# A hybrid four-branch layer on one core: another order of channel tiles, and weights' low parts on VectorE

## The chip, the core and the metric

One Trainium2 chip, of which one core is used. A core has a matrix engine (TensorE, PE), three engines for elementwise work (VectorE or DVE, ScalarE or ACT, GpSimd or POOL) and SyncE (SP), on which most transfers are issued. Each engine runs its own instructions in order; semaphores hold it where it needs another's result. The metric is the device time of one execution in microseconds (us); lower is better.

## The reference

One decoder layer on 2048 prompt tokens with 16 meta tokens ahead of them, and on 8 sample sequences of 4 tokens with saved states. The residual is normalised, then multiplied with a matrix of 1024 rows whose columns feed four branches and their gates:

```python
u = jnp.einsum('btd,de->bte', x, lw['w_in'])
(z_a, xbc, dt_raw, z_b, u_b, z_c, qkv, b_raw, a_raw,
 z_d, q_d, f_d, i_d) = _split_last(u, _IN_SIZES)
```

Branch A is a chunked state-space scan after a causal convolution of 4 taps over `xbc`. Branch B is a diagonal complex scan over `u_b`. Branch C is a gated delta rule: `qkv` goes through a convolution of 4 taps, q and k are L2-normalised per head, and each chunk needs the inverse of a triangular matrix. Branch D is a linear recurrence with a forget gate made of `f_d`. Every branch's result is multiplied by SiLU of its own columns z; the four are joined, multiplied with an output matrix, added to the residual and normalised. All final states are returned too.

## The kernel before, in words

**Stages.** The tokens go through in two halves: 48 (samples and meta tokens) and eight chunks of 128 in the first, eight chunks in the second. Per half, phase 1a normalises and transposes the input and makes the token-major products; phase 1b (`phase1b`, `proj`) makes the other columns, 22 channel tiles of 128 columns. After both halves comes the output phase, 17 chunks in which the last chunks of branches A and C are mixed with the output products.

**A channel tile.** Float32 accuracy is had from two parts of each operand, high and low. `wload` loads a tile's weights (512 KB) into `wr`, of which there is one buffer, copies the high part on ScalarE (L579) and subtracts it on GpSimd for the low part (L580). The next tile's `wload` is called ahead of a tile, and `w` has two buffers, so the parts for tile j+1 can be written once tile j-1 is done. The products run over token blocks of 304, 384 and 384 in the first half, and two of 512 in the second; each block is eight steps of three products (high by high, high by low of x, low of w by high), so 24 products.

**What takes a tile's result.** `conv_tile` (k and q of branch C, v, and x): ScalarE copies the block out (L628 to L635), GpSimd makes the last tap (L639), VectorE adds three more (L641), ScalarE applies SiLU. For k and q the job `l2n` then sums squares (L681, L683), takes a power on GpSimd (L695), scales (L697) and transposes the norm on TensorE. `stream_out` (q, f of branch D, all z): ScalarE only, then a store.

**Order.** The tile order is a list in `phase1b`: k k b b q q l l f f v v x x x x c c a a d d, one letter a tile. k and l are the two pairs of k and q of branch C's convolutions, b c a d the gate columns z of these branches, q and f branch D's, v and x convolutions. The dependent chains (gates, norms, branch B in `right_jobs` and `b_main`, branch D, branch C's inverses) are generators, jobs, that yield an estimate in us of when their next step can start. `poll` is called between the products of `proj` and lets a job go on when the estimate says so. TensorE executes in the order in which this weaving writes it (`keep_in_program_order`); the instructions of the other engines are put in order by the framework's scheduler.

**The hook `last`.** It runs as the first thing of one tile, in place of that tile's own hook: it drains what is left of branch C's inverses, closes the convolutions' buffers, and in the first half starts the second half's input; in the second half it also drains branch D (`right`) and starts the jobs of the remaining chunks (`head`, `c_invs`, `chunks`). Before, that is the first c tile, number 16 counted from 0.

**Branch B.** `b_main` multiplies two arrays of about 1024 columns by cosines on VectorE (L1141, L1150) and their swapped copies, which come by DMA, by sines on GpSimd (L1142, L1151), for four pieces in all. Its setup (`bs_wt`, L1070 to L1072) and the doubling that makes the tables (L956 to L961) run on VectorE early in the first half.

Of the kernel before, what the change touches and what calls it, by code (L numbers as in the profile page):

```python
# [22 lines left out]
F32 = mybir.dt.float32  # L23
# [27 lines left out]
KORD = [0, 1, 4, 5, 6, 7, 2, 3]  # L51
HEAD = META + NS
# [18 lines left out]
class Pinned:  # L71
    """An engine whose instructions don't move ahead of earlier ones."""
# [8 lines left out]
class Chain:  # L81
    """An engine whose instructions issued through here stay in the order in which they are written."""
# [14 lines left out]
class Kern:  # L97
# [12 lines left out]
    # The tensor engine runs in the order in which the kernel is written out. Dependent chains  # L110
    # are generators ("jobs") that yield the time until their next step can start; they are
    # woven between the matrix products of the projections.
# [64 lines left out]
    # ---------------------------------------------------------------- constants  # L177
    def consts(self, cp):
        nc, V, S, G = self.nc, self.V, self.S, self.G
        a = self.a  # L180
# [13 lines left out]
        # sums the two parts of 32 channels of a head  # L194
# [24 lines left out]
    # ---------------------------------------------------------------- phase 1  # L219
    def small_loads(self, cp):  # L220
        """Job: small parameters, and the conv histories of the sample sequences channel-major."""
        a, V = self.a, self.Vp
        yield 8.2
        # channel-major small parameters, through one transpose
# [29 lines left out]
        # HGRN2 lower bound: softmax over the single layer, cumulative sum minus the first entry  # L254
# [18 lines left out]
        for i1 in range(0, 10, 6):  # L273
# [4 lines left out]
            yield 8.5  # L278
# [46 lines left out]
    def phase1a(self, half, xp):  # L325
        """Layer norm and transposition of the input, and the products whose results are wanted token-major.
        The first yield comes before anything that needs the space of xh, xl or the weight ring."""
# [46 lines left out]
        def weights(i, parts):  # L374
            """u | i, dt, a, b: high and low parts."""
# [23 lines left out]
        else:  # L399
            # the first tile waits for as little as possible: one row comes by DMA, the other through the tensor engine  # L400
# [81 lines left out]
    def gates_in(self, half, sp):  # L482
# [3 lines left out]
        o = 1 - half          # chunk 0, the tail, is the first of half 0  # L486
# [14 lines left out]
        # softplus = max(x, 0) + log1p(e), log1p(e) = 2 atanh(e / (2 + e))  # L501
# [20 lines left out]
        # beta = sigmoid  # L522
# [7 lines left out]
        # inclusive cumulative sums inside each chunk, and the chunk totals  # L530
# [20 lines left out]
        if o:  # L551
            # decays of the tail segments, on every partition
# [8 lines left out]
        # rows: 0-7 cumulative logs, 8-15 their exponentials  # L561
# [12 lines left out]
    def wload(self, c0):  # L574
        S, V = self.S, self.V
        w = self.wp.tile([128, 8, 256], F32R, name="w0", bufs=2).rearrange("p k (j c) -> p k j c", j=2)
        raw = self.wp.tile([128, DM], F32, name="wr", bufs=1).rearrange("p (k c) -> p k c", c=128)
        self.ld(raw, self.a["w_in"][0, :, c0:c0 + 128].rearrange("(k p) c -> p k c", p=128))
        S.copy(w[:, :, 0], raw)  # L579
        self.G.tensor_tensor(w[:, :, 1], raw, w[:, :, 0].bitcast(F32), SUB)  # L580
        return w

    def proj(self, tiles):
        """tiles: (first column, per-block consumer, hook at the start); the next tile's weights are made ready first."""
# [20 lines left out]
    def conv_tile(self, i, c0, dst=None, nrm=None):  # L605
        """Causal conv and SiLU of one 128-channel tile, block by block.
        The first block is laid out as 8 x (3 history, 4 sample) | 3 zeros | meta | prompt."""
# [54 lines left out]
    def l2n(self, st, dst, scale, nd, need, key):  # L662
        """Job: L2 normalisation over the channels of a head, for the blocks of a conv tile."""
# [22 lines left out]
        yield 6.1  # L686
# [31 lines left out]
    def decay(self, pool, tag, t, rows0, nh, bufs=None):  # L718
        """exp(acum_i - acum_j) for i >= j of one segment, 0 elsewhere, as [j, head, i]."""
# [10 lines left out]
    def c_pre(self, p):  # L730
        """Job: decayed K K^T and Q K^T of two heads, transposed."""
# [29 lines left out]
    def base_inv(self):  # L761
        """Inverses of the diagonal blocks of I + M, one block to a partition: 32 x 32 in the
        prompt chunks, 16 x 16 in chunk 0, whose segments don't cross multiples of 16."""
# [34 lines left out]
    def stream_out(self, c0, outs, mark=None):  # L798
        """outs: list of (function of (dst, psum)), dram destination)."""
# [18 lines left out]
    def phase1b(self, half, last):  # L818
# [29 lines left out]
        c0, use, _ = zc[0]  # L848
        zc[0] = (c0, use, last)
        tiles = kq[0:2] + zb + qd + kq[2:4] + fd + v + xbc + zc + za + zd  # L850
        yield from self.proj(tiles)

    def conv_states(self):
        """Job: the conv states that go out."""
# [11 lines left out]
    # ---------------------------------------------------------------- branch B  # L866
    def exp_acc(self, pool, dst, x):
        """dst = exp(x) in float32 accuracy, for small tiles."""
# [20 lines left out]
    def b_setup(self, bp, tp):  # L889
# [56 lines left out]
        # powers of lambda, d = 0..8  # L946
# [21 lines left out]
        # rotating frame over chunks of 8  # L968
# [38 lines left out]
        # input matrices  # L1007
# [28 lines left out]
        # output matrices: Xc = (Cr | -Ci), Yc = (-Ci | -Cr)  # L1036
# [25 lines left out]
        # W1 = in-state matrices [(j q), (re n | im n)]  # L1062
# [15 lines left out]
        # block Toeplitz  # L1078
# [17 lines left out]
        # signed multipliers for single steps: h' = re * h + im_s * swap(h)  # L1096
# [17 lines left out]
    def b_main(self, blk, bp, tp):  # L1114
# [8 lines left out]
        for hq in range(2):  # L1123
            yield 4.7 - 95.9 * hq
# [6 lines left out]
        for gh in range(2):  # L1131
            yield 2.0 - gh
# [9 lines left out]
        G.tensor_tensor(Vs, Vs, self.sinT[:, :, 1:65], MUL)  # L1142
# [8 lines left out]
        G.tensor_tensor(Gs, Gs, self.sinT, MUL)  # L1151
# [4 lines left out]
        for hq in range(2):  # L1156
# [14 lines left out]
            yield 2.8 + 0.7 * hq  # L1171
# [112 lines left out]
    # ---------------------------------------------------------------- chunks  # L1284
# [865 lines left out]
```

## Time and profile before

| | us |
|---|---|
| three runs | 1452.39, 1443.35, 1450.69 |
| median | 1450.69 |
| span of the profiled execution | 1448.2 |
| TensorE busy in it | 1294.9 |
| VectorE busy | 934.2 |
| GpSimd busy | 616.3 |
| ScalarE busy | 536.1 |

The profiled execution is given by its span, the time from its first instruction to its last; no other time of it is listed. Its mean granted TensorE clock is 0.936 of full speed. In a row of the trace, L580 is line 580 of the kernel before; names are those of the program, with the tile written left of the arrow.

### The profile page before, as it was taken

The page shows a single profiled execution, that of the slowest core. Times are in us where ns is not written, and L with a number is a line of the kernel's source. Part 1 is how long each engine was busy: PE and PEld are TensorE (multiplying, and loading weights), DVE is VectorE, ACT ScalarE, POOL GpSimd, SP SyncE. Part 2 cuts the span into 40 slices and gives each one's busy share as a digit, 9 for nine tenths or more (in the row PEclk, how much of TensorE's full clock was granted, in tenths as well). Part 3 has the DMA queues.
Part 4 walks back from the last instruction along what each step waited for, and adds up shares of the span by engine and source line. Part 5 has one row for each costly group of instructions (what it writes and reads, how often), then busy time and mean ns, then how long its engine had stood idle before and what let it go on. Part 6 is the DMA issues. An engine that isn't in the chain of part 4 may idle for free. (4 is left out here: it accounts for less than half of the span.)

```text
span 1448.2 us, 23800 instructions
## 1 busy us (share of the span) xinstructions
PE 1294.9 (89%) x8596; PEld 1090.3 (75%) x8596; DVE 934.2 (65%) x2173; ACT 536.1 (37%) x1010; POOL 616.3 (43%) x508
## 2 busy tenths in 40 slices
PE   7984898899898999998996888789997999999997
PEld 6974788878877999877674677677775677777776
DVE  8899524557978549474355789962345676665654
ACT  3224256545214342353543442242434332333211
POOL 4065322524433312152434443441324476676665
PEclk9997999999989999999998899899998899999999
DMA  8511552464337434215534633125649777676333
GB/s 211 192 49 36 127 143 57 140 189 114 106 97 203 145 104 153 77 39 158 157 87 121 201 102 95 44 88 145 177 124 251 196 198 190 198 182 184 111 105 113
DMA packets 259007, 195.79 MB, mean 135 GB/s; under 512 B 70950, under 2 KB 231928, under 8 KB 258873
## 3 DMA queue, kind: packets, MB, share of 16 engines
q1 hardware_dynamic: 258890, 194.28, 47.2%
q8 instruction: 68, 1.11, 0.3%
q14 instruction: 49, 0.39, 0.1%
HBM read 125.01 MB, written 64.31 MB: 131 GB/s over the span
## 5 line engine op out<-in xcount | busy, mean ns | idle before, releaser
L126 PE MATMUL pj<-xh,w 128*128 128x384 f32 (+2 forms) x1760 | 547.8, 379 | 10.8 <-ACT raw L635 5.5
L126 PEld LDWEIGHTS pj<-xh,w 128*128 128x128 f32 x1760 | 339.7, 200 | 57.4 <-issue 11.6
L126 PE MATMUL pj<-xl,w 128*128 128x384 f32 (+2 forms) x880 | 322.8, 367 | 0.0
L126 PEld LDWEIGHTS pj<-xl,w 128*128 128x128 f32 x880 | 176.3, 200 | 12.4 <-issue 0.5
L580 POOL TENSOR_TENSOR w<-wr,w 128x1024 fp32r<-128x1024 f32 x44 | 109.9, 2497 | 85.6 <-ACT w L579 68.0
L641 DVE SCALAR_TENSOR_TENSOR cv<-raw,par,cv 128x384 f32<-128x384 f32 (+2 forms) x150 | 130.5, 872 | 9.5 <-POOL cv L639 8.2
L126 PE MATMUL pj<-woh,o_mh 128*128 128x512 f32 (+2 forms) x280 | 116.6, 416 | 6.3 <-DVE xt L1846 3.2
L126 PE MATMUL pj<-wol,o_mh 128*128 128x512 f32 (+2 forms) x280 | 109.4, 391 | 6.2 <-POOL wol L1817 5.9
L126 PE MATMUL pj<-woh,o_ml 128*128 128x512 f32 (+2 forms) x280 | 109.4, 391 | 0.0
L126 PE MATMUL pj<-w,xh 128*128 128x256 f32 (+3 forms) x544 | 105.2, 295 | 0.0
L639 POOL TENSOR_SCALAR cv<-raw,par 128x384 f32<-128x384 f32 (+2 forms) x50 | 49.3, 986 | 119.0 <-ACT raw L635 95.4
L126 PEld LDWEIGHTS pj<-w,xh 128*128 128x128 f32 (+1 forms) x544 | 84.6, 189 | 1.2 <-ACT xh L88 0.8
L126 PE MATMUL pj<-w,xl 128*128 128x256 f32 (+3 forms) x272 | 78.0, 291 | 0.8 <-DVE xl L88 0.8
L725 POOL TENSOR_TENSOR cdec<-cdec,negm 128x256 f32<-128x256 f32 x32 | 29.4, 921 | 98.6 <-DMA cdec<-rows_d 63.1
L126 PEld LDWEIGHTS pj<-woh,o_mh 128*128 128x128 f32 (+1 forms) x280 | 52.3, 187 | 18.6 <-DVE xt L1846 4.0
L126 PEld LDWEIGHTS pj<-wol,o_mh 128*128 128x128 f32 (+1 forms) x280 | 52.5, 188 | 16.0 <-POOL wol L1817 6.9
L1789 DVE TENSOR_TENSOR y<-y,f_R 128x768 f32<-128x768 f32 (+1 forms) x17 | 27.1, 1591 | 56.0 <-POOL f_R L1788 50.9
L126 PEld LDWEIGHTS pj<-woh,o_ml 128*128 128x128 f32 (+1 forms) x280 | 52.2, 187 | 12.3 <-issue 0.7
L308 POOL TENSOR_TENSOR lnrs<-lnve,mhalf 128x1 f32<-128x1 f32 (+1 forms) x34 | 24.5, 720 | 74.0 <-DVE lnve L88 46.2
L813 ACT ACTIVATE zs<-pj 128x384 f32<-128x384 f32 (+2 forms) x40 | 20.8, 520 | 87.6 <-PE pj L126 72.8
L126 PEld LDWEIGHTS pj<-w,xl 128*128 128x128 f32 (+1 forms) x272 | 51.2, 190 | 1.5 <-DVE xl L88 1.3
L1788 POOL TENSOR_TENSOR f_R<-f_R,f_z 128x768 f32<-128x768 f32 (+1 forms) x17 | 30.2, 1778 | 51.1 <-DMA f_R<-r_d 32.5
(570 smaller groups left out, 2687.8 us busy)
## 6 DMA issues: line engine op xcount, KB each, us to landing
wr<-in_w_in_dram SPq DMA_DIRECT2D x46, 512.0 KB
xt<-in_x_prompt_dram SPq DMA_DIRECT2D x16, 512.0 KB
xn_d<-xt SPq DMA_DIRECT2D x16, 512.0 KB
ma<-cma SPq DMA_DIRECT2D x64, 128.0 KB
xt<-xn_d SPq DMA_DIRECT2D x16, 512.0 KB
out_dram<-xt SPq DMA_DIRECT2D x15, 512.0 KB
f_R<-r_d SPq DMA_DIRECT2D x32, 192.0 KB
cdec<-rows_d SPq DMA_DIRECT2D x32, 128.0 KB
```

Source lines behind the costliest of these rows:

```text
L126: self._pe(self.PE.matmul(out, lhsT, rhs, start=start, stop=stop, **kw), 0.01 + n * (1 if rhs.dtype == F32R else 4) / 2400)
L308: self.G.tensor_tensor(rs[:n], ve[:n], self.mhalf[:n, 0:1], ALU.pow)
L580: self.G.tensor_tensor(w[:, :, 1], raw, w[:, :, 0].bitcast(F32), SUB)
L639: G.tensor_scalar(cv[:, 0:m], raw[:, 3:3 + m], w[3], b, op0=MUL, op1=ADD)
L641: V.scalar_tensor_tensor(cv[:, 0:m], raw[:, k:k + m], w[k], cv[:, 0:m], op0=MUL, op1=ADD)
L725: G.tensor_tensor(d[:n, :, :n], d[:n, :, :n], m[:n, None, :n].to_broadcast([n, nh, n]), ADD)
L813: S.activation(z, p, AF.Silu)
L1788: G.tensor_tensor(R[:, :, :n], R[:, :, :n], z[:, :, :n], MUL)
L1789: V.tensor_tensor(y6[:, 0:6, :n], y6[:, 0:6, :n], R[:, :, :n], MUL)
```

## The change

The two tile orders become tables, one string per half, and the hook gets a place of its own: tile 17, the second c tile, in both halves. The first half starts with a q tile of branch D, an x tile comes right behind the l tiles, and its end is c c a d d a. The second half differs in its end alone, c c a d d a. The subtraction that makes the weights' low part, and the two products with the sines, are issued on VectorE in place of GpSimd. Three estimates in jobs change (the yields below; those of `b_main` keep their values but for one, which was negative and is now 0).

```diff
+ORDER = ["qkkbbqllxffvvxxxccadda", "kkbbqqllffvvxxxxccadda"]
+LAST = [17, 17]
...
-            yield 8.5
+            yield 9.2
...
-        self.G.tensor_tensor(w[:, :, 1], raw, w[:, :, 0].bitcast(F32), SUB)
+        V.tensor_tensor(w[:, :, 1], raw, w[:, :, 0].bitcast(F32), SUB)
...
-        yield 6.1
+        yield 9.0 if half else 6.1
...
-        c0, use, _ = zc[0]
-        zc[0] = (c0, use, last)
-        tiles = kq[0:2] + zb + qd + kq[2:4] + fd + v + xbc + zc + za + zd
+        groups = {"a": za, "b": zb, "c": zc, "d": zd, "q": qd, "f": fd, "k": kq[0:2], "l": kq[2:4], "v": v, "x": xbc}
+        tiles = [groups[g].pop(0) for g in ORDER[half]]
+        c0, use, _ = tiles[LAST[half]]
+        tiles[LAST[half]] = (c0, use, last)
...
-            yield 4.7 - 95.9 * hq
+            yield 0.0 if hq else 4.7
...
-        G.tensor_tensor(Vs, Vs, self.sinT[:, :, 1:65], MUL)
+        V.tensor_tensor(Vs, Vs, self.sinT[:, :, 1:65], MUL)
...
-        G.tensor_tensor(Gs, Gs, self.sinT, MUL)
+        V.tensor_tensor(Gs, Gs, self.sinT, MUL)
```

In instructions: VectorE's order gets 52 operations more, 44 low parts and 8 products with sines, and GpSimd's as many fewer. The lines of the changed kernel are 2 higher than before from L52 on and 4 higher from about L850.

**VectorE, first half, up to the last of branch B's four setup sums** (`bs_wt` of 512 columns; L641 becomes L643, L1072 becomes L1076, and TensorE transposes each sum). Before:

```order
L960 TENSOR_TENSOR bs_l<-sinT,bur 128x256
L960 TENSOR_TENSOR bm_1371<-bui,bur 128x16
L683 TENSOR_REDUCE l2p<-sq 128x2
L641 SCALAR_TENSOR_TENSOR cv<-raw,par,cv 128x384
L1070 TENSOR_TENSOR bs_wt<-bs_X,bpr 128x128 x4
L694 TENSOR_SCALAR l2r<-pq 128x18
L671 MEMSET l2p 128x4
L961 TENSOR_TENSOR sinT<-sinT,bs_l 128x16x16
L961 TENSOR_TENSOR bvi<-bvi,bm_1371 128x16
L681 STREAM_TRANSPOSE sq<-acc 128x256
L641 SCALAR_TENSOR_TENSOR cv<-raw,par,cv 128x384
L1072 TENSOR_TENSOR bs_wt<-bs_wt,bs_wu 128x512
```

and now:

```order
L1075 TENSOR_TENSOR bs_wu<-bs_Y,bpi 128x128 x2
L964 TENSOR_TENSOR bs_l<-sinT,bur 128x256
L963 TENSOR_TENSOR sinT<-cosT,bui 128x16
L643 SCALAR_TENSOR_TENSOR cv<-raw,par,cv 128x384
L1074 TENSOR_TENSOR bs_wt<-bs_X,bpr 128x128 x4
L685 TENSOR_REDUCE l2p<-sq 128x8
L634 COPY cst<-raw 128x24
L965 TENSOR_TENSOR sinT<-sinT,bs_l 128x16x16
L999 COPY bur<-bvr 128x16
L636 COPY raw<-raw 128x3
L643 SCALAR_TENSOR_TENSOR cv<-raw,par,cv 128x328
L1076 TENSOR_TENSOR bs_wt<-bs_wt,bs_wu 128x512
```

Ahead of the second of these sums there stood 10 taps of convolutions (L641), and now 4 (L643); ahead of the third 15 and 7, ahead of the last 18 and 10. Of the 44 low parts (L582), 4 now stand ahead of the last sum. On TensorE the four transposes stand among the same products of tiles 0 to 2 as before, the last of them three products later.

**GpSimd and VectorE, second half, around one call of `b_main`** (`w_...` is a tile's weights, `cdec` and `cma` belong to branch C's decayed products). GpSimd before:

```order
L580 TENSOR_TENSOR w_6631<-wr,w_6631 128x8x128
L695 TENSOR_TENSOR l2r<-l2r,mhalf 128x16
L580 TENSOR_TENSOR w_6761<-wr,w_6761 128x8x128
L725 TENSOR_TENSOR cdec<-cdec,negm 128x256
L580 TENSOR_TENSOR w_6952<-wr,w_6952 128x8x128
L725 TENSOR_TENSOR cdec<-cdec,negm 128x256
L1142 TENSOR_TENSOR b_6934<-b_6934,sinT 128x1024
L725 TENSOR_TENSOR cdec<-cdec,negm 128x256 x2
L1151 TENSOR_TENSOR b_6944<-b_6944,sinT 128x1040
L725 TENSOR_TENSOR cdec<-cdec,negm 128x256 x2
L580 TENSOR_TENSOR w_7116<-wr,w_7116 128x8x128
```

VectorE now, the same call:

```order
L582 TENSOR_TENSOR w_6748<-wr,w_6748 128x8x128
L1716 SCALAR_TENSOR_TENSOR SD<-SD,d_tota,pq 64x64 x4
L696 TENSOR_SCALAR l2r<-pq 128x16
L1144 COPY b_6910<-bH_1937 128x16
L699 TENSOR_SCALAR l2r<-l2r 128x16
L1125 COPY b_6806<-b_6803 128x8x8x16
L704 COPY l2s<-pq 16x128
L715 TENSOR_TENSOR acc<-acc,bc 128x536
L715 TENSOR_TENSOR acc<-acc,bc 128x488
L582 TENSOR_TENSOR w_6888<-wr,w_6888 128x8x128
L1145 TENSOR_TENSOR b_6910<-b_6857,cosT 128x16x64
```

The low parts have left GpSimd's order, where they stood between the powers of the norms (L695) and the decays (L725), and stand in VectorE's between branch B's, the norms' and branch D's instructions.

**TensorE, second half, the end of the convolutions** (`w_8656` is tile 15, the last x tile, `w_8812` tile 16, the first c tile; the other rows are branch D's last chunks). Before:

```order
L126 MATMUL pj<-xl,w_8656 128x512
L126 MATMUL pj<-xh,w_8656 128x512
L120 MATMUL pq<-ident,d_kb 128x128 x2
L126 MATMUL pq<-d_prb,SD 128x128
L126 MATMUL pq<-d_ATb,d_vb 64x128 x2
L126 MATMUL pq<-d_prb,SD 128x128
L126 MATMUL pq<-d_ATb,d_vb 64x128 x2
L126 MATMUL pq<-d_vb,d_ktb 128x128 x2
L120 MATMUL pq<-ident,d_kb 128x128 x2
L126 MATMUL pq<-d_prb,SD 128x128
L126 MATMUL pq<-d_ATb,d_vb 64x128 x2
L126 MATMUL pq<-d_prb,SD 128x128
```

and now:

```order
L122 MATMUL pq<-ident,d_kb 128x128 x2
L128 MATMUL pj<-xh,w_8812 128x512
L128 MATMUL pj<-xl,w_8812 128x512
L128 MATMUL pj<-xh,w_8812 128x512 x2
L128 MATMUL pj<-xl,w_8812 128x512
L128 MATMUL pj<-xh,w_8812 128x512 x2
L128 MATMUL pj<-xl,w_8812 128x512
L128 MATMUL pj<-xh,w_8812 128x512
L128 MATMUL pq<-d_prb,SD 128x128
L128 MATMUL pq<-d_ATb,d_vb 64x128 x2
L128 MATMUL pq<-d_prb,SD 128x128
L128 MATMUL pq<-d_ATb,d_vb 64x128 x2
```

Branch D's last products stood in one piece ahead of tile 16; now they stand between that tile's products. The products of `head` and of the chunk jobs behind them start one tile later, in tile 18.

## Rows read from the trace of the kernel before

**Rows 1.** The page: the span, and each engine's busy time, share and instructions.

```profile
span 1448.2 us, 23800 instructions
PE 1294.9 (89%) x8596; PEld 1090.3 (75%) x8596; DVE 934.2 (65%) x2173; ACT 536.1 (37%) x1010; POOL 616.3 (43%) x508
```

**Rows 2.** Windows: busy time by engine, clock, DMA share, by stretch of the span.

```profile
100.00:125.00 25.00, 14.04 (x65) 12.51 (x63) 23.29 (x81) 9.59 (x20) 15.80 (x28) 0.80 0.08 21
125.00:150.00 25.00, 12.78 (x79) 11.58 (x79) 24.98 (x68) 11.34 (x22) 14.30 (x6) 0.80 0.14 37
750.00:775.00 25.00, 15.81 (x92) 12.44 (x92) 22.99 (x23) 8.28 (x13) 15.62 (x7) 0.84 0.31 85
1150.00:1200.00 50.00, 50.00 (x491) 39.37 (x489) 35.20 (x83) 17.71 (x41) 33.44 (x29) 1.00 0.72 193
```

**Rows 3.** Waits: engine and line, what it waited for, us, times, longest.

```profile
PE pq L120 <- DVE bs_wt L1072: 13.3, 3, 8.3
PE pq L126 <- DVE b L1152: 12.2, 2, 9.2
POOL w L580 <- ACT w L579: 68.0, 16, 10.7
SPq L578 <- POOL w L580: 94.6, 20, 19.1
```

**Rows 4.** Lines: costliest groups, form by form: busy us, mean ns, idle before.

```profile
L580 POOL TENSOR_TENSOR w<-wr,w 128x1024 fp32r<-128x1024 f32 x44 | 109.9, 2497 | 85.6 <-ACT w L579 68.0 <-DMA z_d<-zs 11.0 <-PE pq L126 4.3
L1817 DVE TENSOR_TENSOR wol<-xt,woh 128x1024 fp32r<-128x1024 f32 x6 | 7.7, 1282 | 7.5 <-ACT woh L1816 7.5
L1817 POOL TENSOR_TENSOR wol<-xt,woh 128x1024 fp32r<-128x1024 f32 x2 | 4.7, 2340 | 0.0
L1151 POOL TENSOR_TENSOR b<-b,sinT 128x1040 f32<-128x1040 f32 x4 | 10.2, 2560 | 11.0 <-DMA b<-b 9.8 <-DVE b L1150 1.2
```

**Rows 5.** Timeline (start us, duration us), half 0, 107 to 133 us.

```profile
107.86 2.37 DVE L512 SCALAR_TENSOR_TENSOR g_p<-g_p,g_z 128x72 f32<-128x72 f32 x1
114.98 0.69 PE L126 MATMUL pq<-g_g,triu 128*128 128x64 f32 x2 [7.43 <-DVE g_g L521]
129.35 2.82 DVE L1072 TENSOR_TENSOR bs_wt<-bs_wt,bs_wu 128x512 f32<-128x512 f32 x1
132.23 1.11 PE L120 MATMUL pq<-ident,bs_wt 128*128 128x128 f32 x4 [8.34 <-DVE bs_wt L1072]
```

**Rows 6.** Timeline, four later places: VectorE beside L580, and TensorE after it.

```profile
262.99 2.75 DVE L641 SCALAR_TENSOR_TENSOR cv<-raw,par,cv 128x384 f32<-128x384 f32 x1 [0.49 <-POOL cv L639]
...
761.58 2.82 POOL L580 TENSOR_TENSOR w<-wr,w 128x1024 fp32r<-128x1024 f32 x1
762.07 3.43 DVE L1150 TENSOR_TENSOR b<-b,cosT 128x1040 f32<-128x1040 f32 x1
766.08 2.34 DVE L658 COPY cst<-raw 128x3 f32<-128x3 f32 x1
773.78 0.69 PE L126 MATMUL pq<-Pw,b 128*64 128x128 f32 x4 [9.19 <-DVE b L1152]
...
788.53 2.31 DVE L697 TENSOR_SCALAR l2r<-l2r 128x16 f32<-128x16 f32 x1 [3.02 <-POOL l2r L695]
790.98 0.37 PE L120 MATMUL pq<-ident,l2r 128*16 128x128 f32 x1 [4.57 <-DVE l2r L697]
...
972.61 0.77 PE L126 MATMUL pq<-d_prb,SD 128*128 128x128 f32 x2 [2.96 <-DVE SD L1712]
```

**Rows 7.** Line 641, the convolution's taps: duration in ns, min/median/max, and forms.

```profile
L641 DVE SCALAR_TENSOR_TENSOR cv<-raw,par,cv x150: 532/620/5427, 91.9 to 973.1; 128x384 f32<-128x384 f32 x60, 128x512 f32<-128x512 f32 x60, 128x328 f32<-128x328 f32 x30
```

**Rows 8.** Timeline, the second half's input norm, its first product, its first tile.

```profile
477.43 1.41 DVE L88 SCALAR_TENSOR_TENSOR xt<-xt,lnrs,brow 128x512 f32<-128x512 f32 x2
528.55 1.03 PE L120 MATMUL pq<-ident,xt 128*128 128x128 f32 x8
...
610.17 1.22 PE L126 MATMUL pj<-xh,w 128*128 128x512 f32 x2 [1.70 <-POOL w L580]
```

More of the change, by code (lines that the diff above doesn't have):

```diff
@@ L1131, in b_main @@
         for gh in range(2):
-            yield 2.0 - gh
+            yield 1.0 if gh else 2.0
             p = self.pt()
@@ L1170, in b_main @@
                          p.rearrange("p (g i q) -> p g i q", g=4, i=8), AF.Gelu_apprx_tanh)
-            yield 2.8 + 0.7 * hq
+            yield 3.5 if hq else 2.8
         y5 = tp.tile([128, 2, 64, 8], F32, name="b2")
```

## The prediction

> **What bounds the kernel now.** I read the page first. TensorE is busy for 1294.9 of 1448.2 us, VectorE for 934.2, GpSimd for 616.3 [rows 1]. So TensorE sets the time, and 1448.2 - 1294.9 = 153 us, 10.6% of the span, are what a better order can return, along with what the clock takes. The windows say where these are. In the output phase there is next to nothing: 50.00 of 50.00 us at full clock from 1150 on. In the projections there are holes: 14.04 and 12.78 of 25 us of TensorE at 100 to 150, with VectorE at 23.29 and 24.98, and 15.81 at 750 to 775 with VectorE at 22.99. The granted clock in those windows is 0.80 to 0.84 [rows 2]. The waits then name the releaser: TensorE stands 13.3 us for `bs_wt` and 12.2 us for branch B's rotated state, both made on VectorE [rows 3]. So the question is what holds VectorE, and the timeline answers it. A scaling of 16 columns takes 2.31 us, a copy of 3 columns 2.34 us, branch B's product with cosines 3.43 us [rows 6], a polynomial step of 72 columns 2.37 us and a setup sum 2.82 [rows 5]. The low part is running on GpSimd in these places: it runs from 761.58 to 764.40, the product with cosines starts at 762.07, and ends 1.1 us after it. Likewise a convolution's tap takes 2.75 us at 262.99 [rows 6]; the median of all is 0.62 [rows 7]. An operation on VectorE that begins behind the start of a low part gets going when that ends.
>
> The Trainium skill ("SBUF — State Buffer", section "Who interferes with whom") says of this that VectorE and GpSimd share a pair of ports as an exclusive lock: the one that issues first holds it for its whole instruction, when VectorE has two inputs in SBUF or is in a two-port mode. The rows above agree.
>
> **The change part by part.**
>
> *Low parts, off GpSimd.* 44 operations of 2497 ns, 109.9 us in all, leave GpSimd; as `wol` the same form takes 1.28 us in the mean on VectorE and 2.34 on GpSimd [rows 4]. I take 1.22 us, an undisturbed one, so VectorE gets 54 us. What goes are the stalls. After the first 150 us I find seven on TensorE's path; the taps at 262.99, the product at 762.07, the scaling at 788.53 and a tap ahead of the wait at 972.61 are among them [rows 6]. What each costs is its duration less the undisturbed one: 2.75 - 0.62 = 2.1 us for the tap, and I take that for all (the longest tap is 5.43 us [rows 7], which a longer GpSimd operation holds). 7 x 2.1 = 15 us. In the second half's first tile TensorE waits for a low part itself, 1.70 us [rows 8]; 1.1 of that goes. **-16.**
>
> *Products with sines.* 8 operations; those of 2.56 us [rows 4] become about 1.25. Two of them end a wait of TensorE, the one of 9.19 us at 773.78 [rows 6] among them: -1.3 each. The copy of 2.34 us at 766.08 stood beside such a product, and -2 goes with it. **-5.** The other six lie beside projection products; if that cover is gone they cost VectorE 1.25 us each.
>
> *The first half's start.* With a q tile first, whose result only ScalarE touches, the taps ahead of the second setup sum fall from 10 to 4, ahead of the last from 18 to 10: 8 x 0.62 = 5.0 us. Two stalls, of `g_p` and of the sum, give 2 x 2.1 = 4.2 more [rows 5]. Four low parts stand ahead of the last sum now: +4.9. Net about 4.3, and the seven steps of the norms that move back are not counted. The waits there are 7.43 and 8.34 us and two smaller ones, about 20 together, so there is room for it: **-5**, with bounds 0 (VectorE is full with the tables' doubling in any order) and -18 (nearly all of the holes).
>
> *x behind l, f later, the end in c c a d d a.* Products of equal length change places; a, d and c tiles only store. I cost these at nothing, with 3 us either way for a hole that closes or opens; their cover is the other tiles' products.
>
> *The hook one tile later, first half.* The second half's input norm is ready at 478.84 and first used at 528.55 [rows 8]. Its 22 tiles end at about 528.55, so a tile is less than 528.55 / 22 = 24 us, and 50 us of slack hide it: 0. Its input loads move behind one more weight load on SyncE, under the same slack.
>
> *The hook one tile later, second half.* Branch D's last products get a tile's products between them; of the 2.96 us at 972.61 [rows 6], 2.1 are counted above. Against it, `head` and the chunks have four tiles to hide behind in place of five. The output phase's first weights are waited for anyway. The nearest rows are this 2.96 us as a gain and a pair of chunk products' waits of the same kind as a loss: I take **+2**, bounds -3 and +6.
>
> *The yield 9.0.* The norm's product comes about one block later in the second half. Of the wait of 4.57 us at 790.98 [rows 6], 2.1 are counted, the rest is covered: **-2**. The 9.2 moves a job that waits for loads: 0.
>
> *The clock.* It is low in just the windows with holes: (1 - 0.80) x 50 + (1 - 0.84) x 25 = 14 us [rows 2], against 1.00 where TensorE has no hole. If the holes shrink by half, half of that returns, with one more for the places at 790 and 972: **-8**, bounds 0 and -16.
>
> *What VectorE's queue pays.* The low part now waits in order behind VectorE's work, and that work behind it. What waits in the queue behind it is shown in the order: a table's step, branch B's product, a norm's scaling. Below: 0, if the scheduler has put it where ScalarE's copy is done. Above: GpSimd's 68.0 us of waits for that copy [rows 3], moved over. The nearest row is `wol` on VectorE, 7.5 us of idle time ahead of six [rows 4], 1.25 each; 44 x 1.25 = 55 us, of which 10.6% (TensorE's share of holes) reaches the path: **+6**. SyncE's 94.6 us behind the low parts [rows 3], for the one weight buffer, get 1.3 us shorter at each tile; that load was early, so 0.
>
> Sum: -16 - 5 - 5 + 2 - 2 - 8 + 6 = -28. On the span that makes 1420.2. The median shown is 1450.69, 2.5 above the span, so I predict **1422.7 us**.
>
> By the same page of the Trainium skill the lock also works the other way: a low part on VectorE has two inputs in SBUF, so it can be held by a GpSimd operation, and can hold one. By that rule, with GpSimd busy 43% of the time and 1.2 us to an operation (616.3 / 508), the 44 would lose an estimated 11 us and cost GpSimd up to 23; at 10.6% on the path the sum would come out some 4 us higher, 1427. No row of `wol` decides it: one of six took 1.60 us and five about 1.22.
>
> **The rivals.**
>
> *The holes come back elsewhere (0.17).* VectorE's sum does not fall: 54 + 10 us come, and what the stalls gave was of that size. In the windows where it has 23 to 25 of 25 us, the next link is late in place of the last. Then the clock and the taps give nothing, and what remains is the part in which an operation itself got shorter, -1.1 - 2.6, the one copy, -2, and the yield, -2: **1443 us**. For it speaks 24.98 of 25 us at 125 to 150 [rows 2]; against it, that the stalls stand in other windows too, with VectorE idle behind them.
>
> *Slower: VectorE stands at the low part (0.09).* The part for tile j+1 needs its buffer, free when tile j-1 is done, then the load, then ScalarE's copy. Where VectorE comes to it early, taps, norms and branch B's products stand behind it. Price: GpSimd's 68.0 us moved over, with VectorE at 65% busy: 44 us of work made late. If all of it reaches TensorE and the clock gives nothing back, 1450.7 - 16 - 5 - 5 + 2 - 2 + 44 = **1469 us**. It decides from the point at which 26 of the 44 us come through. Against it: GpSimd had slack, 832 us idle, when it waited there; VectorE mostly comes late, and where it is full the copy will be done.
>
> *More comes back (0.10).* The first half's start gives 18 in place of 5 and the clock 16 in place of 8: 1422.7 - 21 = **1402 us**. For it speaks that all of these holes hang on the one engine that is relieved early; against it, that the tables' doubling stays in the way.
>
> The forecast has 0.64. Less than 1% can't be told from no change here, and 1% is 14.5 us, so the borders are 1436.2 and 1465.2. The forecast and the third rival are faster: 0.74. The first is within: 0.17. The second is slower: 0.09. The range goes from 1398 (the third rival, with 4 us for the tiles whose order I cost at nothing and the second half's end) to 1450, past the first rival with the 6 us by which the end may go the other way; it leaves out the slower case and the tails.
>
> **What would show it.** In the changed kernel's rows: no short operation on VectorE of 2.3 us or more beside a weight's low part; low parts of 1.2 to 1.3 us on VectorE; the wait for `bs_wt` under 10 us, the 9.19 us before branch B's product under 5, the one for the norm near 791 gone; the clock in 100 to 150 above 0.85; VectorE idle ahead of low parts 50 us or less. The forecast is wrong if TensorE's waits sum to the same 150 us under other names, or if ScalarE's copy is the first releaser of VectorE's idle time.

## The result, and the profile after

The changed kernel takes 1434.97 us (median of four runs, 1433.43 to 1438.38) against 1450.16 for the kernel before: a ratio of 0.9888, 95% interval 0.9846 to 0.9929. That is 15 us less, where 28 were forecast; it lies in the range and on the forecast side of 1%, by little: the interval reaches past that border. The profiled execution spans 1432.2 us, 16.0 less than before, at a mean clock of 0.938.

The page after, beside [rows 1]:

```profile
span 1432.2 us, 23785 instructions
PE 1291.8 (90%) x8596; PEld 1088.3 (76%) x8596; DVE 916.9 (64%) x2225; ACT 540.3 (38%) x1012; POOL 496.5 (35%) x456
```

VectorE got 52 operations more and is busy for less: 916.9 against 934.2 us. The groups by line, beside [rows 4, 7], and what the low part waited for:

```profile
L643 DVE SCALAR_TENSOR_TENSOR cv<-raw,par,cv 128x384 f32<-128x384 f32 (+2 forms) x150 | 102.7, 687 | 7.8 <-POOL cv L641 6.8
L582 DVE TENSOR_TENSOR w<-wr,w 128x1024 fp32r<-128x1024 f32 x44 | 54.4, 1237 | 19.4 <-ACT w L581 19.4
```

The low parts cost VectorE 54.4 us and the sines about 10, so 934.2 + 64 - 916.9 = 81 us of other time on VectorE are gone. The taps alone went from a mean of 872 to 687 ns. That is more than the 64, which the first rival took the stalls to be about equal to. VectorE stood idle ahead of low parts for 19.4 us, not for the 55 of the estimate.

Where the span went is seen in windows cut at the same tiles' first products. Columns: window, its length, busy time and instructions of TensorE, weight loads, VectorE, ScalarE and GpSimd, the granted clock, the DMA share, GB/s. Before (tiles 0 to 2, 3 to 7 of the first half; tiles 7 to 15, 16 to 21 of the second; the rest):

```profile
81.90:159.00 77.10, 51.63 (x297) 46.72 (x298) 70.19 (x248) 29.23 (x60) 42.85 (x53) 0.87 0.14 39
159.00:259.50 100.50, 92.81 (x629) 85.50 (x628) 40.65 (x112) 50.39 (x86) 26.94 (x21) 0.93 0.43 114
...
746.30:976.20 229.90, 190.50 (x1013) 153.93 (x1011) 179.59 (x327) 83.10 (x163) 101.71 (x79) 0.89 0.35 106
976.20:1111.70 135.50, 131.86 (x926) 100.65 (x925) 53.66 (x136) 50.62 (x92) 39.80 (x37) 0.93 0.62 162
1111.70:1448.20 336.50, 310.10 (x2376) 241.69 (x2374) 204.16 (x441) 97.58 (x177) 213.85 (x164) 0.96 0.61 169
```

and after:

```profile
81.00:149.00 68.00, 49.91 (x282) 45.00 (x282) 64.53 (x243) 29.69 (x59) 30.34 (x48) 0.87 0.16 47
149.00:259.00 110.00, 96.63 (x647) 89.70 (x646) 45.34 (x126) 48.48 (x85) 16.89 (x17) 0.91 0.41 108
...
744.60:949.60 205.00, 180.56 (x977) 146.53 (x976) 160.15 (x328) 82.21 (x157) 71.61 (x63) 0.93 0.38 114
949.60:1087.20 137.60, 131.79 (x866) 100.50 (x865) 58.96 (x138) 51.29 (x90) 28.86 (x32) 0.90 0.59 155
1087.20:1432.20 345.00, 321.59 (x2471) 248.50 (x2470) 203.70 (x453) 100.97 (x187) 221.10 (x168) 0.96 0.62 169
```

Two gains stand out, and behind each there is a loss. The first tiles take 9.1 us less, the next five 9.5 more. (The numbers are the same, the tiles are not: the first three are k, k, b before and q, k, k after; the eight together are the same.) Tiles 7 to 15 of the second half take 24.9 less, what follows 2.1 and 8.5 more. TensorE's idle time goes the same way in the first pair: from 25.5 to 18.1 us, then from 7.7 to 13.4. In the last pair the instruction counts tell that part of it is no gain: 36 matmuls fewer stand in the shorter window and 60 fewer in the next, and 95 more at the end. The stretches not shown add -0.9, -0.7, -1.9 and +1.4; all together it is the 16.0.

The single places of [rows 5, 6], in lines picked from the timeline after:

```profile
106.22 5.05 POOL L1065 TENSOR_TENSOR Pw<-Pw,bs_w 128x2304 f32<-128x2304 f32 x1
106.30 5.12 DVE L961 TENSOR_TENSOR bs_l<-sinT,bui 128x128 f32<-128x128 f32 x1
...
113.64 0.69 PE L128 MATMUL pq<-g_g,triu 128*128 128x64 f32 x2 [9.08 <-DVE g_g L523]
...
124.34 0.65 PE L122 MATMUL pq<-ident,bs_wt 128*128 128x128 f32 x4 [0.69 <-DVE bs_wt L1076]
...
127.17 2.76 POOL L641 TENSOR_SCALAR cv<-raw,par 128x384 f32<-128x384 f32 x1 [15.90 <-DVE raw L629]
129.97 0.73 DVE L643 SCALAR_TENSOR_TENSOR cv<-raw,par,cv 128x384 f32<-128x384 f32 x1 [0.49 <-POOL cv L641]
130.82 1.00 DVE L1076 TENSOR_TENSOR bs_wt<-bs_wt,bs_wu 128x512 f32<-128x512 f32 x1
...
131.97 1.09 PE L122 MATMUL pq<-ident,bs_wt 128*128 128x128 f32 x4 [3.95 <-DVE l2p L685]
...
240.75 1.22 DVE L582 TENSOR_TENSOR w<-wr,w 128x1024 fp32r<-128x1024 f32 x1
241.88 0.61 DVE L643 SCALAR_TENSOR_TENSOR cv<-raw,par,cv 128x384 f32<-128x384 f32 x1
242.41 0.69 DVE L1125 COPY b<-b 128x1024 f32<-128x1024 f32 x1
243.15 1.12 PE L122 MATMUL pq<-ident,b 128*128 128x128 f32 x4 [4.76 <-DVE b L1125]
...
718.85 0.47 PE L122 MATMUL pq<-ident,b 128*128 128x128 f32 x1 [8.12 <-ACT b L1173]
...
760.81 0.15 DVE L660 COPY cst<-raw 128x3 f32<-128x3 f32 x1
762.16 0.44 PE L128 MATMUL pq<-Pw,b 128*64 128x128 f32 x4 [1.77 <-DVE b L1156]
...
780.62 0.17 DVE L699 TENSOR_SCALAR l2r<-l2r 128x16 f32<-128x16 f32 x1
780.94 0.27 PE L122 MATMUL pq<-ident,l2r 128*16 128x128 f32 x1 [2.56 <-DVE l2r L699]
```

and three lines of before that belong beside them:

```profile
124.00 5.43 DVE L641 SCALAR_TENSOR_TENSOR cv<-raw,par,cv 128x328 f32<-128x328 f32 x1
124.03 5.05 POOL L1061 TENSOR_TENSOR Pw<-Pw,bs_w 128x2304 f32<-128x2304 f32 x1
...
244.24 1.49 PE L120 MATMUL pq<-ident,b 128*128 128x128 f32 x8 [4.22 <-DVE b L1121]
```

The stalls beside low parts went as foreseen: the copy of 3 columns is back at 0.15 us, the scaling at 0.17, the wait of 9.19 us is 1.77. The wait of 8.34 us for the second setup sum is 0.69, but most of it had another cause. The tap of 5.43 us ahead of that sum stood beside one GpSimd instruction of 5.05 us, a product of branch B's setup (L1061, now L1065). That instruction is still on GpSimd. It now runs at 106.22, ahead of the gates, where it holds a step of the tables for 5.12 us.

Other waits took the place of those that went. The gates' wait rose from 7.43 to 9.08 us. At 243 the low part itself now stands in VectorE's queue ahead of the copy that TensorE waits for. At 127 it is GpSimd that is late: its tap takes 2.76 us beside VectorE's work, where the median of these is 0.77, and VectorE waits for it. At 718 TensorE waits 8.12 us for ScalarE, which stands at decays from GpSimd; the like wait before was 3.12. In all TensorE's idle time went from 153.3 to 140.4 us.

### The profile page after: what moved, and what is told of

Same layout as the page of the kernel before. It is cut to its first block, busy times and chain, and to the rows that moved or that the text cites. A ratio compares the mean times of both kernels' runs of the same rounds, so it can differ in the third digit from the quotient of the medians.

```text
span 1432.2 us, 23785 instructions
## 1 busy us (share of the span) xinstructions
PE 1291.8 (90%) x8596; PEld 1088.3 (76%) x8596; DVE 916.9 (64%) x2225; ACT 540.3 (38%) x1012; POOL 496.5 (35%) x456
## 4 chain that ended last, share of the span: by engine, by line
PE 36%; DVE 14%; DMA 11%; POOL 4%; issue 4%; ACT 3%; SPq 1%; POOLq 0%; DVEq 0%; ACTq 0%
PE pj L128 22%; PE pq L128 13%; PE pq L122 2%; DMA f_R<-r_d 2%; DVE cv L643 2%; DMA cdec<-rows_d 2%; DMA r_d<-f_rs 1%; DVE Qa L1670 1%; POOL f_R L1792 1%; DVE acc L791 1%; DVE cdec L789 1%; DMA bc<-nrm 1%; DVE d_ATa L1674 1%; DVE y L1793 1%; DVE w L582 1%
## 5 line engine op out<-in xcount | busy, mean ns | idle before, releaser
L641 POOL TENSOR_SCALAR cv<-raw,par 128x384 f32<-128x384 f32 (+2 forms) x50 | 50.8, 1016 | 203.1 <-ACT raw L637 135.7
L643 DVE SCALAR_TENSOR_TENSOR cv<-raw,par,cv 128x384 f32<-128x384 f32 (+2 forms) x150 | 102.7, 687 | 7.8 <-POOL cv L641 6.8
L582 DVE TENSOR_TENSOR w<-wr,w 128x1024 fp32r<-128x1024 f32 x44 | 54.4, 1237 | 19.4 <-ACT w L581 19.4
L128 PEld LDWEIGHTS pj<-woh,o_ml 128*128 128x128 f32 (+1 forms) x280 | 53.0, 189 | 13.4 <-issue 1.1
L753 DVE SCALAR_TENSOR_TENSOR cma<-pq,nbeta,cdec 128x128 f32<-128x128 f32 (+1 forms) x68 | 23.0, 339 | 46.8 <-ACT cdec L729 32.5
L581 ACT CAST w<-wr 128x1024 fp32r<-128x1024 f32 x44 | 46.0, 1046 | 15.3 <-DMA wr<-in_w_in_dram 10.9
```

The lines of the kernel that those rows point to most:

```text
L128: self._pe(self.PE.matmul(out, lhsT, rhs, start=start, stop=stop, **kw), 0.01 + n * (1 if rhs.dtype == F32R else 4) / 2400)
L582: V.tensor_tensor(w[:, :, 1], raw, w[:, :, 0].bitcast(F32), SUB)
L641: G.tensor_scalar(cv[:, 0:m], raw[:, 3:3 + m], w[3], b, op0=MUL, op1=ADD)
L643: V.scalar_tensor_tensor(cv[:, 0:m], raw[:, k:k + m], w[k], cv[:, 0:m], op0=MUL, op1=ADD)
L753: V.scalar_tensor_tensor(ma[:n, 0, h, :n], pks[h][:n, 0, :n], self.nbeta[:n, t, 2 * p + h:2 * p + h + 1], dec[:n, h, :n], op0=MUL, op1=MUL)
```

## The experiments

Each was timed in five rounds beside the kernel before on the same chip; ratios are to that. The kernel before itself was at 1451.9, 1457.1 and 1454.7 us on the three chips, so ratios are compared, not times.

**1. Low parts alone.** Edit, in the kernel before:

```diff
-        self.G.tensor_tensor(w[:, :, 1], raw, w[:, :, 0].bitcast(F32), SUB)
+        V.tensor_tensor(w[:, :, 1], raw, w[:, :, 0].bitcast(F32), SUB)
```

> The kernel before with the 44 low parts on VectorE and nothing else. Theory 1 (the low parts on GpSimd held VectorE, and that is what pays): their own terms of the sum, -16 of stalls, +6 of queue, and half of the clock's -8, so -14: 1436 us; VectorE's busy time falls, and no short operation of 2.3 us stands beside a low part. Rival (the tile order and the hook pay, the stalls only move): within 3 us of before, 1447 to 1453, with TensorE's waits at the same 150 us. If VectorE stands at the low parts it is over 1455.

Measured: 1432.24 us, 0.9865 (0.9837 to 0.9892). The one line gives 20 us, all that the whole change gives.

```profile
span 1428.8 us, 23798 instructions
PE 1287.6 (90%) x8596; PEld 1082.1 (76%) x8596; DVE 920.4 (64%) x2217; ACT 534.4 (37%) x1008; POOL 521.3 (36%) x464
L580 DVE TENSOR_TENSOR w<-wr,w 128x1024 fp32r<-128x1024 f32 x44 | 56.9, 1294 | 34.4 <-ACT w L579 34.3
```

Less its 56.9 us of low parts VectorE has 863.5, so the same 2173 instructions take 934.2 - 863.5 = 71 us less. Most of this can be placed. In the kernel before, 32 of VectorE's instructions that overlap a low part are over 0.5 us longer than the like ones (their median in seven traces with low parts on VectorE): 62 us in sum, 1.9 each.

The second setup sum has no wait in this run, at 128.86, although the tile order is that of before; the gates wait 16.21 us. The 5 us instruction of GpSimd now holds the gates' own product, of 72 columns:

```profile
114.93 5.27 POOL L1061 TENSOR_TENSOR Pw<-Pw,bs_w 128x2304 f32<-128x2304 f32 x1
115.23 5.06 DVE L521 TENSOR_TENSOR g_g<-sp,g_ac 128x72 f32<-128x72 f32 x1
```

**2. All but the low parts.** Edit, in the changed kernel: the line above the other way.

> The changed kernel with the 44 low parts back on GpSimd; order, hook, yields and the products with sines as changed. Theory 1: it loses what the low parts brought, 1435 + 14 = 1449 us, and the operations of 2.3 to 2.9 us beside low parts are back. Rival (order and hook pay): it keeps nearly all, 1435 to 1438. If gains don't add (the holes come back elsewhere), it lies between, near 1442, and so does the kernel before with low parts alone.

Measured: 1469.2 us, 1.0117 (1.0090 to 1.0143): slower than before by 17, which none of the three expected. Order, hook, estimates and sines, without the low parts, are a loss. The long instructions are back, as expected: again 32 beside low parts, 62 us longer in sum. VectorE loses no more to them than before, so the loss of 17 us lies in where they fall, or in the rest of the change.

**3. The first half's order as before.** Edit, in the changed kernel:

```diff
-ORDER = ["qkkbbqllxffvvxxxccadda", "kkbbqqllffvvxxxxccadda"]
+ORDER = ["kkbbqqllffvvxxxxccaadd", "kkbbqqllffvvxxxxccadda"]
```

> The changed kernel with the first half's tiles in the order of before (k k b b q q l l f f v v x x x x c c a a d d), the hook still at tile 17. By the prediction's terms the first half's start is worth 5 and some of the clock: 1435 + 7 = 1442 us. By the account of the two traces, stage by stage, the start gains 9 us up to tile 3 and gives 8 back before tile 8, so the order nets 1 to 2 us: 1436. In both the wait for the setup sums is over 8 us again.

Measured: 1439.61 us, 0.9919 (0.9895 to 0.9943). Between the two expectations, and its interval overlaps that of the changed kernel. What both expected of the waits did not come: those for the setup sums are 1.00, 2.86 and 3.15 us, none over 8. So the new order was not needed to take the 8.34 us away.

**4. The second half's hook at tile 16.** Edit: `LAST = [17, 16]`.

> The changed kernel with the second half's hook back at the first c tile (16), so branch D's last products stand in one piece ahead of it again and the remaining chunks start one tile earlier. By the prediction's term (+2 for the later hand-over, with 3 us of wait counted elsewhere): 1432 to 1434 us. Rival (weaving branch D's end under a tile is a good part of the 19 us that the stretch from 757 to 976 us gained): 1440 to 1445, with TensorE's waits ahead of tile 16 back.

Measured: 1432.91 us, 0.9884 (0.9855 to 0.9913): no different from the changed kernel. Its windows, cut at the same tiles:

```profile
750.10:961.40 211.30, 184.79 (x1012) 147.82 (x1011) 165.79 (x338) 85.68 (x164) 74.22 (x65) 0.93 0.39 114
961.40:1100.90 139.50, 135.41 (x927) 102.74 (x926) 58.44 (x142) 51.21 (x94) 31.30 (x35) 0.90 0.61 157
1100.90:1436.80 335.90, 311.81 (x2376) 243.30 (x2374) 202.21 (x440) 97.28 (x176) 214.35 (x164) 0.96 0.61 170
```

Tiles 7 to 15 take 6 us more than in the changed kernel, with 35 matmuls back, and the end 9 less, with the 95 gone again. The one wait that stands out is 2.01 us for branch D's state, at 959.24 with the hook at 16; the changed kernel has none there. The later hand-over moves work and hides none on balance, as far as ratios that are known to 0.3% tell.

**5. The length of GpSimd's instruction.** Edit, in the kernel before, low parts left on GpSimd:

```diff
-        self.G.tensor_tensor(w[:, :, 1], raw, w[:, :, 0].bitcast(F32), SUB)
+        for k in range(8):
+            self.G.tensor_tensor(w[:, k, 1], raw[:, k], w[:, k, 0].bitcast(F32), SUB)
```

> The kernel before, low parts on GpSimd, but each cut in eight instructions of 128 columns. If a low part holds VectorE for the length of its own instruction (lock per instruction), an operation of VectorE that meets one waits for 0.3 to 0.5 us at most, no short operation of 2.3 us is left, and the time goes most of the way to that of low parts on VectorE: 1435 to 1442 us, less the eight starts. If the two engines simply share bandwidth, or if GpSimd's many instructions follow each other without a gap for VectorE, the stalls stay at 2.3 us and the time at 1450 or above it.

Measured: 1438.46 us, 0.9897 (0.9856 to 0.9939). The same subtractions on the same engine, cut in eight, give most of the gain. Its timeline beside a low part:

```profile
268.62 7.32 POOL L581 TENSOR_TENSOR w<-wr,w 128x128 fp32r<-128x128 f32 x8
268.68 0.81 DVE L642 SCALAR_TENSOR_TENSOR cv<-raw,par,cv 128x384 f32<-128x384 f32 x1 [0.41 <-POOL cv L640]
269.41 0.17 DVE L695 TENSOR_SCALAR l2r<-pq 128x18 f32<-128x18 f32 x1
...
269.96 2.45 DVE L1146 TENSOR_TENSOR_SCAN b<-rdec,b 128x1040 f32<-128x1040 f32 x1
...
273.00 1.49 DVE L1151 TENSOR_TENSOR b<-b,cosT 128x1040 f32<-128x1040 f32 x1
```

A tap that starts just behind the first piece takes 0.81 us; the like one at 262.99 took 2.75 [rows 6]. Here GpSimd waits in its turn: eight pieces of 0.45 us take 7.32 us, the longest of the 44 tiles (the shortest is 3.35). Its two longest pieces, 2.46 and 1.45 us, stand beside the scan and the product shown. The page of this run has VectorE at 904.8 us, 29 below before, and GpSimd at 697.8, 82 above. Each tile's low part now takes longer than the 2.4 us that the single instruction takes in the median, and the gain comes all the same, so it is not owed to quicker low parts.

**6. An order changed without a reason.** Edit, in the kernel before: `yield 8.5` made `yield 9.2`.

> The kernel before with the one estimate 8.5 made 9.2, and nothing else: 26 rows of TensorE's order differ, and some hundred of VectorE's, which the scheduler puts elsewhere. It is there to measure what another order without a reason is worth. If small rearrangements are neutral: 1447 to 1455 us. If the scheduler's order is a lottery that moves the time by itself: 5 us or more away from before, in either direction, and differences of that size between the other runs then show nothing about their edits.

Measured: 1464.6 us, 1.0057 (1.0026 to 1.0087). Eight us for an edit with no purpose.

**7. The sines back on GpSimd.** Edit, in the changed kernel: `V.tensor_tensor` made `G.tensor_tensor` in the two lines of the sines.

> The changed kernel with the eight products with sines back on GpSimd. By the prediction's term of -5 they were worth it on VectorE: 1440 us. Rival (VectorE is the fuller engine, and with the low parts gone GpSimd has room, so moving these 8 more cost what it gave): 1431 to 1436. The stalls of short copies beside them, 2.3 us each, should be seen again in either case.

Measured: 1435.94 us, 0.9860 (0.9828 to 0.9892), as good as with them on VectorE. The local wait is longer: 4.05 us ahead of branch B's product at 761.08, against 1.77 in the changed kernel. There VectorE waits 2.27 us for the product with sines, which takes 3.37 us beside a low part on VectorE. Of the stalls that were to return, three did beside the eight products: a copy of 3 columns takes 0.92 us, one of 24 columns 1.95 and a tap 2.69.

**8. The estimates of before.** Edit, in the changed kernel: 9.2 made 8.5, and `9.0 if half else 6.1` made 6.1.

> The changed kernel with the two estimates of before (8.5, and 6.1 in both halves). By the prediction's term of -2: 1437 us, with a longer wait for the norm's product near 780. Rival (the norm's product one block later makes the products that need it late): 1430 to 1433.

Measured: 1443.2 us, 0.9904 (0.9878 to 0.9929). The ratio overlaps the changed kernel's; with experiment 6 in mind it says nothing of the yields' sense. The norm's product waits 3.20 us at 787.49, against 2.56 at 780.94 in the changed kernel.

**9. Low parts with the new orders and hook.** Edit: experiment 7 and 8 together in the changed kernel.

> The kernel before with the low parts on VectorE and the new tile orders with the hook at tile 17; products with sines on GpSimd and estimates as before. If the low parts carry the gain and order and hook are worth nothing or cost 3 to 5 us: a ratio of 0.987 to 0.992 to before, about that of the low parts alone (0.9865). If order and hook add their terms (-5, +2 and the clock): 0.980 or less.

Measured: 1441.58 us, 0.9909 (0.9874 to 0.9945): in the range of the first expectation, and clear of the 0.980 that the terms of order and hook would have given.

**10. Low parts with q first.** Edit, in the kernel of experiment 1:

```diff
+        if half == 0:
+            tiles = qd[0:1] + kq[0:2] + zb + qd[1:2] + kq[2:4] + fd + v + xbc + zc + za + zd
```

> The kernel before with the low parts on VectorE and one q tile put first in the first half; everything else as before. The stage account of the runs so far shows the stretch of the first three tiles 4 to 5 us shorter with q first, and the tiles 3 to 14 some 14 us longer where x and f were moved too. If the loss comes of x and f: 4 us better than low parts alone, ratio 0.983. If what q first gives is only deferred (the norms and taps that it moves come back in tiles 3 to 7): within 2 us of low parts alone, 0.985 to 0.988.

Measured: 1441.47 us, 0.9912 (0.9881 to 0.9944): worse than both expectations, and no better than low parts alone. Its first two windows, and those of experiment 1 behind them:

```profile
80.70:150.30 69.60, 49.41 (x282) 44.76 (x281) 64.85 (x243) 32.20 (x61) 31.98 (x48) 0.85 0.16 44
150.30:257.90 107.60, 95.59 (x646) 88.30 (x645) 45.17 (x127) 49.02 (x86) 17.45 (x18) 0.90 0.43 110
```

```profile
80.90:153.60 72.70, 49.45 (x299) 44.46 (x298) 67.14 (x254) 27.57 (x59) 37.99 (x50) 0.86 0.17 47
153.60:254.00 100.40, 92.72 (x629) 85.20 (x628) 40.46 (x116) 49.25 (x85) 14.07 (x16) 0.93 0.44 114
```

With x and f where they were, q first wins 3.1 us in three tiles and loses 7.2 in the next five. That is the pattern of the changed kernel, so x and f are not its cause.

**11. The new order with low parts cut in eight on GpSimd.** Edit: experiment 5's lines in the changed kernel.

> The changed kernel with the low parts back on GpSimd, each in eight instructions of 128 columns. In one instruction each it took 1469 us, 17 above before. If that loss came of the length of GpSimd's single instruction: most of the 34 us between it and the changed kernel come back, ratio 0.990 to 0.996. If it came of the order itself (work on GpSimd in any form stands ahead of what TensorE needs): it stays above before, 1.005 or more.

Measured: 1451.36 us, 0.9978 (0.9945 to 1.0011). Some 20 of the 34 us that lie between experiment 2 and the changed kernel come back: less than the first expectation, but not the second. So the larger part of those 34 us is owed to the length of the single instruction.

**12. Experiment 6's edit with low parts on VectorE.**

> The kernel before with low parts on VectorE, and the one estimate 8.5 made 9.2: a second sample of an order changed without a reason. Made in the kernel before, the same edit cost 8 us (ratio 1.0057). If the spread of such changes is 5 to 8 us: a ratio between 0.981 and 0.992. If low parts on VectorE owe their 20 us to a lucky order alone, this one falls back to 0.995 or above.

Measured: 1440.38 us, 0.9903 (0.9866 to 0.9939), within the spread that was expected.

All ratios in one view, by where the low parts are made:

| order and the rest | GpSimd, one instruction | GpSimd, eight | VectorE |
|---|---|---|---|
| of before | 1 | 0.9897 | 0.9865 |
| of before, one estimate moved | 1.0057 | | 0.9903 |
| as changed | 1.0117 | 0.9978 | 0.9888 |
| as changed but for one part (3, 4, 7, 8) | | | 0.9919, 0.9884, 0.9860, 0.9904 |
| q first; orders and hook only (10, 9) | | | 0.9912, 0.9909 |

Nine kernels with low parts on VectorE lie between 0.986 and 0.992, whatever their order. In each row the low part's move gives 1.4%, 1.5% and 2.3%, more than the one reasonless edit moved in its two samples (0.6%, and 0.4%, which is within noise). Down the columns the rest of the change goes up three times, by 0.2, 0.8 and 1.2%. With low parts on VectorE this is inside that spread: that the rest costs something there is not shown, nor that it gains nothing at all, but by the two intervals a gain above some 4 us is excluded. On GpSimd it costs more than the two samples moved; which of its parts does, stays open.

## Why the prediction came out as it did

The time lies in the range, which was wide, but the sum did not come true as it was made up. The 1435 us are 12 above the forecast's 1422.7 and 8 below the first rival's 1443.

**Low parts: right in mechanism, too small.** The terms were -16 for the stalls and +6 for the queue, with about half the clock's -8: -14. Alone they measured -20, and -22 and -33 in the other two rows of the table. The mis-sized term is the -16, and in it the count: I took seven stalls that end a wait of TensorE, by 2.1 us, where 32 instructions are held, by 1.9 us in the mean. That the others make TensorE late too, through the instructions behind them, is the likeliest reading; no run separates the two kinds.

**The queue: too dear.** VectorE's idle time ahead of low parts is 19.4 us, for which I took 55 from six operations in another stage. The slower rival took its 44 us from GpSimd's 68.0 us of waits for ScalarE's copy; on VectorE these waits are the 19.4 us, and 34.4 in experiment 1. But the low part's own 1.22 us does stand ahead of what TensorE waits for, as at 243, where the wait went from 4.22 to 4.76 us instead of falling by 2.1. The sum had no term for that.

**The first half's start: -5 forecast, returned two tiles later.** This step failed. The windows show 9.1 us less and then 9.5 more. The waits that the term named, for the gates and the four setup sums, went from 20.8 us together to 14.9, so its size was right for its place. But what was moved out of the first three tiles, a tile's taps and a tile's norms, is not less work, and tiles 3 to 7 pay. Their waits went from 7.7 to 13.4 us, and no single one makes the difference: 1.8 for branch C's decayed products, 2.3 and 1.3 for results of ScalarE are new. Q first alone shows the same pattern (experiment 10). The order's excerpt showed the taps ahead of the sum fall from 10 to 4; I priced what left the window, not where it went.

The term also missed the largest single piece of the 8.34 us. It counted the sum's own stall of 2.1, but the tap of 5.43 us ahead of it, 4.8 over the median, stood beside GpSimd's product of 5.05 us, which no part of the change touches. In each of ten orders whose traces were compared, one VectorE instruction beside this product takes 4.2 to 5.4 us, whatever its size: a copy of 24 columns 5.01 in experiment 10, the gates' product 5.06 in experiment 1. Only its place moves with the order.

**Sines: -5 forecast, nothing found.** The wait of 9.19 us shrank to 1.77, and is 4.05 with the sines on GpSimd, so 2.3 of it are the sines', where 1.3 was given. The total does not tell: 2.3 us in one place are below what the scheduler's rearrangement moves. The step that failed is to carry local gains into the sum with no cost for VectorE's ten us; what took them back is not shown.

**The later hook: +2 forecast, 0 measured.** Within its bounds, and in line with the reason given: the wait at branch D's end, 2.01 us, is covered, and the end of the kernel loses about what the stretches before it gain. **The yields:** -2 forecast, not separable. **The clock:** -8 forecast; its mean went from 0.936 to 0.938 only, and at 100 to 150 us it was 0.73 and 0.93, not above 0.85 throughout.

**In short** the sum credited the low parts with -14 and the rest with -14. The runs give the low parts 20 to 33, and the rest nothing, or a cost that the table bounds. So part of the agreement is luck: a term that was too small and a part that gave nothing partly made up for each other. The first rival, holes that come back elsewhere, was half the truth: it is what became of the rest's part.

**The rule on the lock**, which stood beside the sum (the Trainium skill, "SBUF — State Buffer", "Who interferes with whom": the one that issues first has the shared ports for its whole instruction, and the other is blocked), is borne out by experiment 5: VectorE's tap waits 0.2 us (0.81 - 0.62) when GpSimd's instruction is short, 2.1 when it is long, with the same bytes moved. The estimate of 11 us for low parts held by GpSimd was too high: their mean is 1.237 us against a median of 1.218, so 44 x 0.019 = 0.8 us. The other direction exists: GpSimd's remaining operations take 496.5 us where 616.3 - 109.9 - 19.4 = 487 were left, 9.5 more; in experiment 1 they take 521.3 where 506.4 were left, 14.9 more.

## What to carry to other kernels

Where two engines hold each other up, look at the lengths of instructions first: cutting one long one in eight, on the same engine, gave 15 us, and moving it gave 20. Compare an engine's instructions with the same ones undisturbed: the excess (62 us on 32 instructions here) shows stalls that no wait of the critical engine names. When a wait goes away, look whether what caused it is gone or has moved, as GpSimd's product of 5 us did. When the instruction order comes from a scheduler, run an edit without a purpose beside the real ones; here one moved 8 us, so a reordering that promises less than that needs a stage account that ends at zero work moved, not one window that got shorter.

## What had not been expected of the hardware

With GpSimd's instruction cut in pieces, both engines lose time to each other. The pieces, 0.448 us at the shortest, take a mean of 0.580 each over the run: 204 us for 352, some 46 more than undisturbed. VectorE's 904.8 us are 29 below before, but 41 above the 863.5 that it has without low parts beside it (experiment 1). So the cut did not end the mutual hold; it made each one short, and that gave most of the time back.

```profile
L581 POOL TENSOR_TENSOR w<-wr,w x352: 448/463/2463, 76.5 to 1051.5; 128x128 fp32r<-128x128 f32 x176
```

The columns are the shortest, median and longest duration in ns, and the first and last start in us.
